# A streaming encoder step on one Trainium2 core: S5 maps all on VectorE, memory rows split by an accumulating DMA, both PSUM banks of a scan read at once

## The chip, the core and the metric

The kernel runs on one NeuronCore of a Trainium2 chip. The metric is the device time of one execution in microseconds, median of several runs. The engines in the profile are TensorE (PE, with its weight loads as PEld), VectorE (DVE), ScalarE (ACT), GpSimd (POOL) and SyncE (SP), which only issues DMAs. SBUF is the on-chip memory, PSUM the eight accumulator banks that TensorE writes.

## The reference, cut to what matters

One step of a two-layer encoder, for 512 prompt and 32 sample tokens (544 columns) of width 1024. Layer 0 mixes tokens by an S5 state-space branch (48 groups of 16 channels, 64 complex states each) with a GLU, beside a 4-head attention into 256 memory tokens; layer 1 by multi-head latent attention and the same kind of memory attention. After each comes a gated conv FFN of width 2816. What the change touches:

```python
bu_re = einsum('blgc,gnc->blgn', ug, bb_re)          # inputs to the states, complex
h_re, h_im = associative_scan(complex_affine, ...)   # h = lambda * h + bu over the tokens
y = einsum('blgn,gcn->blgc', h_re, c_re) - einsum('blgn,gcn->blgc', h_im, c_im) + d_skip * u
out = gelu(y) * sigmoid(gelu(y) @ w_glu + b_glu)

m = rms_norm(mem[None], mem_norm_g)                  # memory rows, for both layers
k, v = split(einsum('lbmd,ldk->lbmk', m, w_mem_kv))
```

## The kernel before, in words

Matmuls keep fp32 accuracy by splitting each operand into a high and a low part of a shorter type and adding three products. For weights, `weights` (L226) loads the raw block on SP's queue, ScalarE writes the high part (L231) and the negated raw block into the low part (L232), and a DMA on POOL's queue adds the raw block onto it (L233). `gemm_part` (L316) issues the three products, each on two halves of 272 columns. Three buffers exist for each of raw, high and low.

The program is written in Tile: a scheduler orders each engine's instructions by priorities from a table (ORDER, L67) that the sections of the program name with `pri` and `unit`; the engines then run their lists in that order and wait on semaphores. Pools of SBUF buffers (F, with fx merged into it; R for row pairs; BG and BS for four PSUM banks each) set how far work runs ahead. The order inside an engine's list is therefore a result of priorities, buffers and the scheduler, and a change to one place moves instructions elsewhere.

Layer 0 works over six chunks m of eight groups (loop at L1033). For each chunk, `s5_wv` (L661) builds the input maps: per real and imaginary half two products and a sum of 128x512 (L670, L672), one half on DVE and one on POOL. `s5_wvt` (L676) turns them by PE. `s5_wc` (L688) builds the output maps: per half of the groups two products and a sum of 128x576 (L697, L699), again one on DVE and one on POOL; then matmuls (L701) make the short convolution kernels, which go through POOL (L706, L708) and a DMA round trip in `s5_kernel`. `s5_scan` (L746) lets PE write two PSUM banks (L753), rotates them by four DVE operations of 128x276 (L763, L764), sums (L766, L767), scans (L771), rotates back (L774) and combines (L780, L781); two small memsets are on DVE (L758, L768). `s5_output` (L786) makes the outputs (L792, L793, transposes L804).

`mem_kv` (L333) runs between these steps as filler, in eight pieces (four blocks u of the memory rows times two layers l). A piece scales its rows by the norm's gain into a high part on ScalarE (L344) and a low part on DVE (L345), two of each of 128x256, loads a w_mkv block, and issues its matmuls (L350). Two pairs of row buffers serve the eight pieces. When all is summed, keys are finished with L398 and the transposes L404.

Then come memory attention, the GLU (L1094), the output projection, the first conv FFN, and layer 1: its norm (sums of squares L260 and L262, a chain of small DVE operations, the broadcast L284), the latents in `finish_latents`, which also multiplies the rotary tables by gains on POOL (L1216, L1218), the attention (scores L1557, transposes L1582, values L1593), the output projection and the second FFN. L324 is every weight matmul, L331 and L866 its evacuations. L966 to L968 are the evacuations of layer 0's input projection into the S5 inputs. L640 to L643 build the S5 tables by doubling, and L358 sums the squares of the memory rows on POOL.

```python
        for gh, e in enumerate((V, P)):
            g = 8 * m + 4 * gh
            for o, x in ((c, 0), (d, 1)):
                e.tensor_tensor(o[gh], view(q["cc"], [[16, 4], [0, 9], [1, 16]], 16 * (48 * x + g)),
                                view(q["prd"], [[1, 4], [48, 9], [0, 16]], 432 * x + g), ALU.mult)
            e.tensor_tensor(c[gh], c[gh], d[gh], ALU.add)
```

Of the kernel before, what the change touches and what calls it, by code (L numbers as in the profile page):

```python
# [9 lines left out]
F32 = mybir.dt.float32  # L10
F32R = mybir.dt.float32r
# [66 lines left out]
class Slots:  # L78
# [59 lines left out]
def body(ctx, tc, A, O):  # L138
# [10 lines left out]
    B = slots(pp, 8, F32, 512, "bank")  # L149
# [40 lines left out]
    B.put(b)  # L190
    F.put(warm)
# [142 lines left out]
    def mem_kv(fm, rm, bm, b1, dst):  # L334
        ps = [[bm.get(512) for _ in range(2)] for _ in range(2)]
        acc = fm.get(2, NMEM)
        for u in range(4):
            mt = fm.get(2, NMEM)
            nc.sync.dma_start(mt, A["mem"][:, 2 * u:2 * u + 2, :])
            for l in range(2):  # L340
                hi, lo = rm.get(2, NMEM), rm.get(2, NMEM)
                for k2 in range(2):
                    g = gcol("mem", l * KD + 2 * u + k2)
                    S.activation(hi[:, k2], mt[:, k2], AF.Copy, scale=g)  # L344
                    V.scalar_tensor_tensor(lo[:, k2], mt[:, k2], g, hi[:, k2].bitcast(F32), ALU.mult, ALU.subtract)  # L345
# [318 lines left out]
    def s5_wv(q, m, fs):  # L664

        a = [fs.get(4, 8, 16) for _ in range(2)]
        b = [fs.get(4, 8, 16) for _ in range(2)]
        for ri, e in enumerate((V, P)):
            for o, x, pw in ((a, ri, "pr"), (b, 1 - ri, "pi")):
                e.tensor_tensor(o[ri], view(q["bb"], [[16, 4], [0, 8], [1, 16]], 16 * (NPR * x + 4 * m)),  # L670
                                view(q[pw], [[1, 4], [NPR, 8], [0, 16]], 4 * m), ALU.mult)
            e.tensor_tensor(a[ri], a[ri], b[ri], ALU.add if ri else ALU.subtract)  # L672
        fs.put(*b)
        return a

    def s5_wvt(a, fs, bs):  # L676
        wv = []
        for ri in range(2):
            pb = bs.get(512)
            for i in range(4):  # L680
                T.transpose(pb[:, 128 * i:128 * i + 128], a[ri][:, i].rearrange("p a b -> p (a b)"), ident)
# [1120 lines left out]
```

## Time and profile before

| what | value |
|---|---|
| three runs | 1459.69, 1460.1, 1463.19 us; median 1460.1 |
| the profiled execution's own time | 1460.42 us |
| its span, first to last instruction | 1458.6 us |
| mean granted TensorE clock | 0.979 of full speed |
| busy: PE | 1409.9 us (97%) |
| busy: DVE, ACT, POOL | 738.8, 753.4, 408.7 us |
| 0 to 36.9 us: loads, first norm, start of the input projection | PE 26.66 us busy |
| 36.9 to 180.0 us: rest of the projection, S5 chunks, memory keys and values | PE 120.07, DVE 134.21 us busy |
| 180.0 to 196.5 us: last S5 output, keys, start of memory attention | PE 14.94 us busy |
| 196.5 to 690 us: memory attention, GLU, projection, first FFN | PE 492.8 us busy |
| 690 to 1010 us: layer 1 up to its attention's end | PE 313.54 us busy |
| 1010 to 1458.6 us: projection, second FFN | PE 441.84 us busy |

A busy share over the whole span mixes these stages. It is read stage by stage: where PE is busy throughout, no other engine's work shows in the time; where it is not, its waits name the engine that it waits for.

### The profile page before, as it was taken

To read this page: it belongs to the slowest core of one execution; us is meant where nothing else is said; L and a number is where in the kernel's file an instruction comes from. 1 tells how busy PE (TensorE), PEld (TensorE's weight loads), DVE (VectorE), ACT (ScalarE), POOL (GpSimd) and SP (SyncE) were. 2 spreads that over 40 slices of the span, in tenths; PEclk is the share of its full clock that TensorE was granted. 3 is DMA by queue.
4 is the path that set the end of the run, shared out by engine and by line. 5 is a ranking of instruction groups with operands and counts; after the bars stand their busy time and mean duration, and the time that the engine had idled before them with its cause. 6 is when DMAs were issued, how large, how long until landed. Compare 5 with 4: busy or idle time off the path is not lost.

```text
span 1458.6 us, 26919 instructions
## 1 busy us (share of the span) xinstructions
PE 1409.9 (97%) x10693; PEld 1315.7 (90%) x10693; DVE 738.8 (51%) x1801; ACT 753.4 (52%) x1247; POOL 408.7 (28%) x649
## 2 busy tenths in 40 slices
PE   7888899999999999999999999999999999999998
PEld 6777679999999999999989987557999999999998
DVE  7989852355513551355247755663355513551351
ACT  6455475555534553456554554654555534553452
POOL 3546532322211221124226422332322211221121
PEclk8997899999999999999999999999999999999999
DMA  8665547778888878878751342011778887888875
GB/s 246 139 145 133 118 117 161 158 175 173 175 175 174 178 173 175 176 161 184 162 132 60 97 121 48 26 30 42 163 177 175 180 176 171 178 177 171 176 155 138
DMA packets 71902, 214.77 MB, mean 147 GB/s; under 512 B 8128, under 2 KB 17312, under 8 KB 71776
## 3 DMA queue, kind: packets, MB, share of 16 engines
q0 software_dynamic: 27616, 96.16, 37.5%
q1 hardware_dynamic: 43008, 114.80, 27.1%
q10 hardware_dynamic: 1152, 2.10, 0.5%
q8 instruction: 84, 1.38, 0.4%
q14 instruction: 42, 0.34, 0.1%
HBM read 207.41 MB, written 5.61 MB: 146 GB/s over the span
## 4 chain that ended last, share of the span: by engine, by line
PE 82%; DVE 2%; issue 1%; ACT 1%; DMA 1%; POOL 0%; DVEq 0%; POOLq 0%; ACTq 0%
PE bank L324 65%; PE bank L1309 2%; PE bank L1557 2%; PE bank L1396 2%; PE bank L1593 1%; PE bank L1510 1%; PE bank L1484 1%; PE bank L1582 1%; PE bank L1192 1%; PE bank L482 1%; PE bank L520 1%; PE bank L1424 1%; DMA wlo<-i_w_f 0%; PE bank L510 0%; PE bank L1365 0%
## 5 line engine op out<-in xcount | busy, mean ns | idle before, releaser
L324 PE MATMUL bank<-rc,whi 128*128 128x272 f32 x3728 | 627.5, 289 | 0.9 <-DVE fx L393 0.7
L324 PEld LDWEIGHTS bank<-rc,whi 128*128 128x128 f32 x3728 | 528.3, 188 | 4.2 <-issue 2.1
L324 PE MATMUL bank<-rc,wlo 128*128 128x272 f32 x1864 | 388.3, 288 | 0.0
L231 ACT ACTIVATE whi<-wraw 128x1024 fp32r<-128x1024 f32 (+2 forms) x186 | 191.1, 1028 | 360.6 <-issue 314.2
L324 PEld LDWEIGHTS bank<-rc,wlo 128*128 128x128 f32 x1864 | 293.7, 188 | 1.9 <-issue 1.6
L324 PE MATMUL bank<-g,whi 128*128 128x272 f32 x1408 | 234.9, 289 | 0.0
L233 POOL DMA_DIRECT2D wlo<-i_w_f x136 | 117.3, 863 | 304.9 <-ACT wlo L232 303.0
L324 PEld LDWEIGHTS bank<-g,whi 128*128 128x128 f32 x1408 | 198.8, 188 | 0.6 <-ACT g L216 0.4
L232 ACT ACTIVATE wlo<-wraw 128x1024 fp32r<-128x1024 f32 (+2 forms) x186 | 189.0, 1016 | 9.9 <-PE bank L350 9.3
L324 PE MATMUL bank<-g,wlo 128*128 128x272 f32 x704 | 146.0, 288 | 1.6 <-DMA wlo<-i_w_f 1.6
L852 DVE SCALAR_TENSOR_TENSOR fa<-fa,gp,fa 128x546 f32<-128x546 f32 x88 | 69.4, 789 | 139.4 <-ACT fa L851 139.4
L866 DVE TENSOR_TENSOR h<-bank,h 128x272 f32<-128x272 f32 x96 | 38.2, 435 | 173.0 <-PE bank L324 172.4
L324 PEld LDWEIGHTS bank<-g,wlo 128*128 128x128 f32 x704 | 110.5, 188 | 1.9 <-DMA wlo<-i_w_f 1.9
L844 DVE TENSOR_TENSOR fa<-bank,fa 128x272 f32<-128x272 f32 x88 | 38.9, 442 | 82.6 <-PE bank L324 78.1
L851 ACT ACTIVATE fa<-fa,gp 128x546 f32<-128x546 f32 x88 | 73.1, 831 | 12.9 <-DVE fa L846 12.9
L853 DVE SCALAR_TENSOR_TENSOR fa<-fa,gp,fa 128x546 f32<-128x546 f32 x88 | 69.4, 789 | 3.1
L848 POOL COPY fa<-gp 128x2 f32<-128x2 f32 x88 | 19.0, 220 | 169.4 <-DVE g L217 105.1
L892 ACT ACTIVATE fa<-fa 128x546 f32<-128x546 f32 x44 | 29.1, 662 | 71.3 <-DVE fa L853 71.3
L849 POOL COPY fa<-fa 128x4 f32<-128x4 f32 x88 | 18.0, 204 | 166.5 <-DVE fa L846 166.5
L324 PE MATMUL bank<-ra,whi 128*128 128x272 f32 x256 | 49.5, 314 | 13.7 <-DVE fa L968 5.5
L324 PEld LDWEIGHTS bank<-ra,whi 128*128 128x128 f32 x256 | 40.5, 207 | 16.8 <-DVE fa L968 6.2
L216 ACT ACTIVATE g<-fa 128x544 fp32r<-128x544 f32 x44 | 28.9, 658 | 37.3 <-DVE fa L894 37.3
(691 smaller groups left out, 2057.2 us busy)
## 6 DMA issues: line engine op xcount, KB each, us to landing
wraw<-i_w_f SPq DMA_DIRECT2D x120, 512.0 KB
wlo<-i_w_f POOLq DMA_DIRECT2D x120, 512.0 KB, 7.3
wraw<-i_w_out SPq DMA_DIRECT2D x16, 512.0 KB
wlo<-i_w_out POOLq DMA_DIRECT2D x16, 512.0 KB, 7.4
wraw<-i_w_in SPq DMA_DIRECT2D x14, 512.0 KB
wlo<-i_w_in POOLq DMA_DIRECT2D x14, 512.0 KB, 7.5
wraw<-i_w_f SPq DMA_DIRECT2D x16, 384.0 KB
wlo<-i_w_f POOLq DMA_DIRECT2D x16, 384.0 KB, 6.1
```

The costliest lines, as they stand in the source:

```text
L231: S.activation(hi, raw, AF.Copy)
L232: S.activation(lo, raw, AF.Copy, scale=-1.0)
L233: P.dma_start(lo, ap, accum_op=ALU.add)
L324: T.matmul(ps[q][:, :c], ww, xx[:, c0:c0 + c], start=k == 0 and i == 0, stop=k == n - 1 and i == 2)
L844: V.tensor_tensor(u[:, 2:274], ps[0][:, :272], rb[:, :272], ALU.mult)
L851: S.activation(y, u[:, 2:548], AF.Identity, scale=gcol("cw", 3 * ci + 2), bias=gcol("cb", ci))
L852: V.scalar_tensor_tensor(y, u[:, 1:547], gcol("cw", 3 * ci + 1), y, ALU.mult, ALU.add)
L853: V.scalar_tensor_tensor(y, u[:, 0:546], gcol("cw", 3 * ci), y, ALU.mult, ALU.add)
L866: V.tensor_tensor(h[m][:, c0:c0 + cc], ps[qd][:, :cc], h[m][:, c0:c0 + cc], ALU.add)
L1309: T.matmul(b[:, :384], xx[:, 128 * t:128 * t + 128], ww[:, 384 * (k % 2):384 * (k % 2) + 384], start=k == 0 and i == 0, stop=k == NM - 1 a ...
L1396: T.matmul(b[:n, 256 * j:256 * j + 256], xx[:, c0:c0 + n], ww[:, k], start=k == 0 and c == 0, stop=k == 1 and c == 2)
L1557: T.matmul(b[:, :n], qt[:, 128 * t:128 * t + 128], kt[:, :n], start=True, stop=True)
```

## The change

`s5_wv` puts all six operations of a chunk on DVE, still 128x512. `s5_wc` puts its work on DVE in three operations of 128x1152, in place of three of 128x576 on each engine. Both take their buffers from a new pool FD of double width (four slots, and two made of `big`), and fx shrinks from 13 to 8. In `mem_kv`, POOL scales the rows into a new buffer `gm` (two operations of 128x256), ScalarE copies it to the high part and, negated, to the low part (128x512 each), and an accumulating DMA on POOL's queue, from SBUF to SBUF, adds `gm` onto the low part; the two DVE operations L345 of a piece go. `s5_scan` takes two adjacent banks (`get2`; the bank tiles are now 1024 wide) and reads both with one operation of 552 columns, two such in place of four; its two memsets go to POOL. The sums of squares of the first norm are all on DVE. The rotary products move from `finish_latents` to the start of layer 1. They and two small memsets of layer 1 keep their place in the program's order.

```diff
+    def get2(self):
+        for t in self.free:
+            for u in self.free:
+                a, b = t[:], u[:]
+                if a.tensor.name == b.tensor.name and b.offset == a.offset + 512:
+                    self.free = [x for x in self.free if x is not t and x is not u]
+                    return a, b, view(a, [[512, 2], [1, 512]])
+        raise AssertionError("no two banks side by side")
     def retire(self, *tiles):
...
     def slots(pool, n, dt, w, name):
...
-    B = slots(pp, 8, F32, 512, "bank")
+    B = Slots([])
+    for i in range(4):
+        t2 = pp.tile([128, 1024], F32, name=f"bank{i}")
+        for j in range(2):
+            B.free.append(t2[:, 512 * j:512 * j + 512])
+            B.own(B.free[-1])
+    banks = list(B.free)
...
             for l in range(2):
-                hi, lo = rm.get(2, NMEM), rm.get(2, NMEM)
+                hi, lo, gm = rm.get(2, NMEM), rm.get(2, NMEM), fm.get(2, NMEM)
                 for k2 in range(2):
-                    g = gcol("mem", l * KD + 2 * u + k2)
-                    S.activation(hi[:, k2], mt[:, k2], AF.Copy, scale=g)
-                    V.scalar_tensor_tensor(lo[:, k2], mt[:, k2], g, hi[:, k2].bitcast(F32), ALU.mult, ALU.subtract)
+                    P.tensor_scalar(gm[:, k2], mt[:, k2], gcol("mem", l * KD + 2 * u + k2), 0.0, ALU.mult, ALU.add)
+                S.activation(hi, gm, AF.Copy)
+                S.activation(lo, gm, AF.Copy, scale=-1.0)
+                P.dma_start(lo, gm, accum_op=ALU.add)
+                fm.put(gm)
...
-    def s5_wv(q, m, fs):
-        a = [fs.get(4, 8, 16) for _ in range(2)]
-        b = [fs.get(4, 8, 16) for _ in range(2)]
-        for ri, e in enumerate((V, P)):
+    def s5_wv(q, m, fd):
+        a, b = fd.get(2, 4, 128), fd.get(2, 4, 128)
+        for ri in range(2):
             for o, x, pw in ((a, ri, "pr"), (b, 1 - ri, "pi")):
-                e.tensor_tensor(o[ri], view(q["bb"], [[16, 4], [0, 8], [1, 16]], 16 * (NPR * x + 4 * m)),
+                V.tensor_tensor(o[:, ri].rearrange("p i (s c) -> p i s c", s=8),
+                                view(q["bb"], [[16, 4], [0, 8], [1, 16]], 16 * (NPR * x + 4 * m)),
                                 view(q[pw], [[1, 4], [NPR, 8], [0, 16]], 4 * m), ALU.mult)
-            e.tensor_tensor(a[ri], a[ri], b[ri], ALU.add if ri else ALU.subtract)
-        fs.put(*b)
+            V.tensor_tensor(a[:, ri], a[:, ri], b[:, ri], ALU.add if ri else ALU.subtract)
+        fd.put(b)
...
-    def s5_wvt(a, fs, bs):
+    def s5_wvt(a, fs, fd, bs):
...
             for i in range(4):
-                T.transpose(pb[:, 128 * i:128 * i + 128], a[ri][:, i].rearrange("p a b -> p (a b)"), ident)
+                T.transpose(pb[:, 128 * i:128 * i + 128], a[:, ri, i], ident)
...
             wv.append(w)
-        fs.put(*a)
+        fd.put(a)
...
-    def s5_wc(q, m, fs, bs):
+    def s5_wc(q, m, fs, fd, bs):
...
         pk = bs.get(512)
-        c = [fs.get(4, 9, 16) for _ in range(2)]
-        d = [fs.get(4, 9, 16) for _ in range(2)]
-        for gh, e in enumerate((V, P)):
-            g = 8 * m + 4 * gh
-            for o, x in ((c, 0), (d, 1)):
-                e.tensor_tensor(o[gh], view(q["cc"], [[16, 4], [0, 9], [1, 16]], 16 * (48 * x + g)),
-                                view(q["prd"], [[1, 4], [48, 9], [0, 16]], 432 * x + g), ALU.mult)
-            e.tensor_tensor(c[gh], c[gh], d[gh], ALU.add)
+        c, d = fd.get(8, 9, 16), fd.get(8, 9, 16)
+        for o, x in ((c, 0), (d, 1)):
+            V.tensor_tensor(o, view(q["cc"], [[16, 8], [0, 9], [1, 16]], 16 * (48 * x + 8 * m)),
+                            view(q["prd"], [[1, 8], [48, 9], [0, 16]], 432 * x + 8 * m), ALU.mult)
+        V.tensor_tensor(c, c, d, ALU.add)
+        fd.put(d)
+        for gh in range(2):
             for i in range(4):
-                T.matmul(pk[32 * i:32 * i + 32, 128 * gh:128 * gh + 128], view(q["xq"], [[1, 32]], 16 * (g + i)),
-                         c[gh][:, i, 0:8].rearrange("p a b -> p (a b)"), start=True, stop=True)
-        fs.put(*d)
+                T.matmul(pk[32 * i:32 * i + 32, 128 * gh:128 * gh + 128],
+                         view(q["xq"], [[1, 32]], 16 * (8 * m + 4 * gh + i)),
+                         c[:, 4 * gh + i, 0:8].rearrange("p a b -> p (a b)"), start=True, stop=True)
...
     def s5_scan(q, m, u, wv, fs, bs):
...
-        ps = [bs.get(512) for _ in range(2)]
+        *ps, vv = bs.get2()
...
         S.activation(mul, view(q["mag"], [[0, 2], [1, 4], [0, 70]], 4 * m), AF.Copy)
-        V.memset(view(mul, [[70, 8], [65, 2]]), 0.0)
-        cs, sn = (q["tab"][:, i, 4 * m:4 * m + 4] for i in range(2))
+        P.memset(view(mul, [[70, 8], [65, 2]]), 0.0)
         w, t0, t1 = fs.get(2, 4, 70), fs.get(2, 4, 70), fs.get(2, 4, 70)
-        for ri in range(2):
-            v = ps[ri][:, :276].rearrange("p (a b) -> p a b", a=4)
-            V.tensor_tensor(t0[:, ri, :, 1:], v, cs[:, :, 1:], ALU.mult)
-            V.tensor_tensor(t1[:, ri, :, 1:], v, sn[:, :, 1:], ALU.mult)
+        P.memset(w[:, :, :, 0:1], 0.0)
+        for t, i in ((t0, 0), (t1, 1)):
+            V.tensor_tensor(t[:, :, :, 1:], view(vv, [[512, 2], [69, 4], [1, 69]]),
+                            view(q["tab"], [[0, 2], [70, 4], [1, 69]], 70 * (NPR * i + 4 * m) + 1), ALU.mult)
...
         V.tensor_tensor(w[:, 1, :, 1:], t0[:, 1, :, 1:], t1[:, 0, :, 1:], ALU.subtract)
-        V.memset(w[:, :, :, 0:1], 0.0)
...
     for k in range(2, KD):
-        (V if k % 2 else P).tensor_tensor(sqs[k % 2], sqs[k % 2], sqs[k], ALU.add)
+        V.tensor_tensor(sqs[k % 2], sqs[k % 2], sqs[k], ALU.add)
...
     lr = exr.enter_context(tc.tile_pool(name="l0b", bufs=1, reuse_waits="tile"))
-    R, fx = slots(lr, 4, F32R, 512, "rb"), slots(lr, 13, F32, FW, "fx")
+    R, fx, FD = slots(lr, 4, F32R, 512, "rb"), slots(lr, 8, F32, FW, "fx"), slots(lr, 4, F32, 2 * FW, "fd")
...
     F.merge(fx)
-    F.merge(Slots([big[:, FW * i:FW * i + FW] for i in range(NX)]))
+    FD.merge(Slots([big[:, 2 * FW * i:2 * FW * i + 2 * FW] for i in range(2)]))
...
     qsT = [lp.tile([96, 128], F32, name=f"qsT{g}") for g in range(3)]
+    kcs = lp.tile([128, 320], F32, name="kcs")
+    for i, nm in enumerate(("cos", "sin")):
+        for o, nr in ((view(kcs, [[32, 5], [1, 32]], 160 * i), "kr"), (gcs[:, i], "qr")):
+            tc.keep_in_program_order(P.tensor_tensor(o, view(cn, [[32, 5], [1, 32]], CN[nm][0]),
+                                                     view(grow(nr), [[0, 5], [1, 32]]), ALU.mult))
...
     ssl = lp.tile([128, 10], F32, name="ssl")
-    V.memset(ssl[:, 8:10], 1.0)
+    tc.keep_in_program_order(V.memset(ssl[:, 8:10], 1.0))
...
                         view(r1, [[1, 5], [0, 2]]), ALU.mult)
-        kcs = lp.tile([128, 320], F32, name="kcs")
-        for i, nm in enumerate(("cos", "sin")):
-            P.tensor_tensor(view(kcs, [[32, 5], [1, 32]], 160 * i), view(cn, [[32, 5], [1, 32]], CN[nm][0]),
-                            view(grow("kr"), [[0, 5], [1, 32]]), ALU.mult)
-            P.tensor_tensor(gcs[:, i], view(cn, [[32, 5], [1, 32]], CN[nm][0]), view(grow("qr"), [[0, 5], [1, 32]]),
-                            ALU.mult)
...
     def key_norms():
         ss = sm(108, "kss", 1)
-        V.memset(ss, 1.0)
+        tc.keep_in_program_order(V.memset(ss, 1.0))
```

The rest passes the pools on to the functions (FD to `s5_wv`, `s5_wvt` and `s5_wc`) and gives the output maps back to FD. Line numbers of the new kernel are higher by 15 to 19.

How this moves instructions stands in the engines' lists. The first place is POOL's list at the start of the S5 chunks (`cc`, `bb`: output and input factors; `pr`, `pi`, `prd`: powers; `wlo`: low weight parts; `rb`: row pairs; `kp`: kernels). Before:

```order
L1218 TENSOR_TENSOR gcs<-cn,gr 128x160
L697 TENSOR_TENSOR fa_73<-cc_396,prd 128x576
L670 TENSOR_TENSOR fa_76<-bb_395,pi 128x512
L670 TENSOR_TENSOR fa_74<-bb_395,pr 128x512
L697 TENSOR_TENSOR fx_853<-cc_396,prd 128x576
L672 TENSOR_TENSOR fa_74<-fa_74,fa_76 128x512
L699 TENSOR_TENSOR fa_73<-fa_73,fx_853 128x576
L697 TENSOR_TENSOR fa_92<-cc_396,prd 128x576
L697 TENSOR_TENSOR fx_853<-cc_396,prd 128x576
L699 TENSOR_TENSOR fa_92<-fa_92,fx_853 128x576
L233 DMA wlo_99<-i_w_in 128x1024
```

Now:

```order
L360 TENSOR_SCALAR fx_853<-fx_852,gp 128x256 x2
L250 DMA wlo_97<-i_w_in 128x1024
L363 DMA rb_846<-fx_853 128x512
L250 DMA wlo_95<-i_w_in 128x1024
L250 DMA wlo_96<-i_w_in 128x1024
L250 DMA wlo_97<-i_w_mkv 128x1024
L250 DMA wlo_95<-i_w_mkv 128x1024
L250 DMA wlo_96<-i_w_mkv 128x1024
L726 TENSOR_TENSOR kp<-kp,fa_72 128x2x16
L724 TENSOR_TENSOR fa_72<-cn,sp_141 128x32
L250 DMA wlo_97<-i_w_mkv 128x1024
L360 TENSOR_SCALAR fx_854<-fx_852,gp 128x256 x2
```

The map products are gone from POOL; in their stead stand scalings (L360), accumulating row DMAs (L363), weight issues (L250, which was L233) and memsets of the scan (L776), one behind the other.

The second place is PE's list at the end of S5, where `L793` and `L792` are the last chunk's outputs, `L350` the last memory matmuls and `L404` the transposes of the keys. Before:

```order
L792 MATMUL bank_63<-fx_861,big 69x128
L404 MATMUL bank_68<-cn,fa_71 128x128 x4
L350 MATMUL bank_65<-whi_96,rb_852 128x512
L793 MATMUL bank_63<-fx_853,fx_860 69x128
L792 MATMUL bank_63<-fx_861,big 69x128
L793 MATMUL bank_63<-fx_853,fx_860 69x128
L792 MATMUL bank_63<-fx_861,big 69x128
L793 MATMUL bank_63<-fx_853,fx_860 69x128
L430 MATMUL bank_68<-cn,fa_74 128x2 x4
```

Now, where L808 and L809 were L792 and L793, L423 was L404, L820 was L804 and L341 was L324:

```order
L808 MATMUL bank_65<-fa_67,fa_70 69x128
L809 MATMUL bank_65<-big,fx_856 69x128
L808 MATMUL bank_65<-fa_67,fa_70 69x128
L809 MATMUL bank_65<-big,fx_856 69x128
L341 MATMUL bank_63<-rc_1876,whi_94 128x272 x2
L341 MATMUL bank_63<-rc_1877,whi_94 128x272 x2
L820 MATMUL bank_66<-cn,fx_852 128x69 x4
L423 MATMUL bank_65<-cn,fx_855 128x128 x4
L341 MATMUL bank_63<-rc_1876,wlo_97 128x272
L820 MATMUL bank_66<-cn,fa_68 128x69 x4
```

The transposes of the keys moved behind the last output matmuls and behind four weight matmuls.

The third place is PE's list at the start of layer 1, from the sums of squares to the broadcast. Before (the lines left out are L324 as well):

```order
L260 MATMUL bank_67<-cn,fa_72 128x1 x4
L262 MATMUL bank_67<-cn,fa_72 32x1 x4
L324 MATMUL bank_65<-rc_1903,whi_96 128x272
L324 MATMUL bank_68<-rc_1903,whi_96 128x272
L324 MATMUL bank_65<-rc_1904,whi_96 128x272
L324 MATMUL bank_68<-rc_1904,whi_96 128x272
...
L324 MATMUL bank_65<-rc_1909,wlo_99 128x272
L284 MATMUL bank_70<-cn,nr_0_306 128x128 x4
L285 MATMUL bank_63<-cn,nr_0_306 128x32
```

Now (L277 and L279 are the sums, L301 and L302 the broadcast):

```order
L277 MATMUL bank_64<-cn,fa_75 128x1 x4
L279 MATMUL bank_64<-cn,fa_75 32x1 x4
L341 MATMUL bank_63<-rc_1876,whi_92 128x272
L301 MATMUL bank_66<-cn,nr_0_302 128x128 x4
L302 MATMUL bank_65<-cn,nr_0_302 128x32
L341 MATMUL bank_63<-rc_1877,whi_92 128x272
L341 MATMUL bank_63<-rc_1876,wlo_95 128x272
```

Before, 23 weight matmuls stood between the sums and the broadcast; now one does.

## Rows read from the trace of the kernel before

**Rows 1.** Windows: us; busy of PE, PEld, DVE, ACT, POOL; PE clock; DMA share; GB/s.

```profile
36.90:180.00 143.10, 120.07 (x975) 102.87 (x976) 134.21 (x230) 74.65 (x158) 78.82 (x73) 0.87 0.57 132
180.00:196.50 16.50, 14.94 (x114) 12.72 (x112) 11.63 (x56) 12.37 (x32) 4.26 (x8) 1.00 0.54 146
230.00:690.00 460.00, 459.91 (x3646) 457.85 (x3643) 193.80 (x387) 236.94 (x287) 102.39 (x178) 1.00 0.80 174
```

**Rows 2.** Waits of PE, 36.9 to 180 us: us in total, times, longest.

```profile
PE bank L324 <- DVE fa L968: 5.5, 3, 3.6
PE bank L350 <- DVE rb L345: 3.9, 4, 1.7
PE bank L701 <- DVE fa L699: 3.5, 1, 3.5
```

**Rows 3.** Timeline of DVE, 62 to 87 us: start, us, line, operation.

```profile
62.83 0.68 DVE L670 TENSOR_TENSOR big<-bb,pi 128x512 f32<-128x512 f32 x1
63.43 0.95 DVE L640 TENSOR_TENSOR big<-tab,p_sc 128x768 f32<-128x768 f32 x1
...
86.05 0.44 DVE L763 TENSOR_TENSOR fx<-bank,tab 128x276 f32<-128x276 f32 x1
86.41 0.43 DVE L764 TENSOR_TENSOR fx<-bank,tab 128x276 f32<-128x276 f32 x1
```

**Rows 4.** Timeline of DVE, 48 to 64 us.

```profile
52.32 1.33 DVE L640 TENSOR_TENSOR big<-tab,p_sc 128x96 f32<-128x96 f32 x1
...
54.95 0.43 DVE L966 TENSOR_TENSOR fa<-bank,fa 128x272 f32<-128x272 f32 x1
```

**Rows 5.** Timeline of POOL, the same time.

```profile
51.81 1.74 POOL L672 TENSOR_TENSOR fa<-fa,fa 128x512 f32<-128x512 f32 x1
...
54.88 1.23 POOL L697 TENSOR_TENSOR fa<-cc,prd 128x576 f32<-128x576 f32 x1
```

**Rows 6.** Lines by form, DVE, 36.9 to 180 us: busy us, mean ns | idle.

```profile
L345 DVE SCALAR_TENSOR_TENSOR rb<-fa,gp,rb 128x256 fp32r<-128x256 f32 x12 | 8.7, 737 | 0.0
```

**Rows 7.** Lines by form, POOL, 36.9 to 180 us.

```profile
L697 POOL TENSOR_TENSOR fx<-cc,prd 128x576 f32<-128x576 f32 x7 | 10.1, 1442 | 2.4 <-DVE rb L345 2.3
L233 POOL DMA_DIRECT2D wlo<-i_w_mkv x8 | 7.0, 875 | 11.3 <-ACT wlo L232 10.7 <-issue 0.3 <-ACT fa L806 0.3
...
L358 POOL TENSOR_TENSOR fx<-fx,fx 128x512 f32<-128x512 f32 x2 | 3.3, 1674 | 0.0
...
L699 POOL TENSOR_TENSOR big<-big,fx 128x576 f32<-128x576 f32 x1 | 1.9, 1912 | 0.0
```

**Rows 8.** Timeline of POOL, 204 to 208 us.

```profile
204.93 0.48 POOL L498 TENSOR_SCALAR fa<-fa,zri 128x256 f32<-128x256 f32 x1
```

**Rows 9.** Timeline of DVE, line 1094.

```profile
205.68 0.93 DVE L1094 SCALAR_TENSOR_TENSOR fa<-fa,fa 128x544 f32<-128x544 f32 x1 [0.21 <-ACT fa L1092]
...
213.88 0.72 DVE L1094 SCALAR_TENSOR_TENSOR fa<-fa,fa 128x544 f32<-128x544 f32 x1
```

**Rows 10.** Lines by form, ACT, 36.9 to 180 us.

```profile
L344 ACT ACTIVATE rb<-fa,gp 128x256 fp32r<-128x256 f32 x12 | 5.8, 506 | 2.8 <-PE bank L350 2.0 <-DVE rb L345 0.9
```

**Rows 11.** DMA issues, 0 to 250 us: count, KB each, median us to landing.

```profile
wlo<-i_w_mkv POOLq DMA_DIRECT2D x8, 512.0 KB, 7.1
...
o_mem_k<-fa POOLq DMA_DIRECT2D x1, 256.0 KB, 2.5
```

**Rows 12.** Timeline of PE at the end of S5.

```profile
186.33 0.63 PE L404 MATMUL bank<-cn,fa 128*128 128x128 f32 x4 [0.93 <-DVE fa L398]
```

**Rows 13.** Timeline of PE at the start of layer 1.

```profile
695.07 0.24 PE L262 MATMUL bank<-cn,fa 128*32 128x1 f32 x8
...
698.23 0.60 PE L284 MATMUL bank<-cn,nr 128*128 128x128 f32 x4
```

**Rows 14.** Windows in and at the end of layer 1's attention, columns as in rows 1.

```profile
740.00:990.00 250.00, 243.61 (x1555) 188.94 (x1553) 155.10 (x532) 131.91 (x357) 88.15 (x153) 0.98 0.25 69
990.00:1010.00 20.00, 19.93 (x104) 12.43 (x104) 8.87 (x33) 7.96 (x24) 3.69 (x9) 1.00 0.00 0
```

More of the change, by code (lines that the diff above doesn't have):

```diff
@@ L190, in body @@
     B.put(b)
+    B.free = banks
     F.put(warm)
@@ L792, in s5_output @@
                 T.matmul(o, u[:, 4 * gh + i, :], kk[gh][:, i], start=True, stop=False)
-                T.matmul(o, hh[:, 4 * gh + i, 0:69], wc[gh][:, i, 1:9].rearrange("p a b -> p (a b)"), start=False,
+                T.matmul(o, hh[:, 4 * gh + i, 0:69], wc[:, 4 * gh + i, 1:9].rearrange("p a b -> p (a b)"), start=False,
                          stop=True)
@@ L916, in body @@
     R = slots(lr, 16, F32R, NT, "ra")
-    NX = 4
-    big = lp.tile([128, NX * FW], F32, name="big")
+    big = lp.tile([128, 4 * FW], F32, name="big")
     BG, BS = B.take(4), B.take(4)
@@ L982, in out0 @@
         yield from s5_output(us[m], wc, kk, hs[m], y, F, BS)
-        F.put(us[m], hs[m], *wc, *kk)
+        F.put(us[m], hs[m], *kk)
+        FD.put(wc)
         ys.append(y)
@@ L1023, in products @@
         with pri("s5_wv"):
-            return s5_wv(q5, m, F)
+            return s5_wv(q5, m, FD)
     def turn(a):
         with pri("s5_wvt"):
-            wvs.append(s5_wvt(a, F, BS))
+            wvs.append(s5_wvt(a, F, FD, BS))
     def step(g):
@@ L1038, in do_wc @@
         with pri("s5_wc"):
-            wcs.append((s5_wc(q5, m, F, BS), s5_kernel(q5, m, F)))
+            wcs.append((s5_wc(q5, m, F, FD, BS), s5_kernel(q5, m, F)))
     do_wc(0)
@@ L1068, in body @@
     P.dma_start(O["ssm"], q5["hf"])
-    F.retire(big, *fxs)
+    F.retire(*fxs)
     exr.close()
```

## Prediction, made before the changed kernel was run

> **What bounds the kernel now.** I began with the windows by stage. TensorE (PE) is busy 97% of the whole span, so the time can only go down where PE stands idle or at a low clock. The first conv FFN leaves it next to nothing: 459.9 of 460 us, 0.126 us a matmul [rows 1]. The stretch from 36.9 us (row scales ready) to 180.0 us (last scan instruction) is another matter: PE is busy 120.1 of 143.1 us, at a granted clock of 0.87, while VectorE (DVE) is busy 134.2 us, 94% [rows 1]. The waits of PE in this stretch say on whom: the three longest entries, 12.9 us together, are all ended by DVE results [rows 2]. So DVE bounds this stretch.
>
> Then I asked why DVE is so busy. Where POOL runs nothing beside it, the distance from one start to the next is 0.60 us for 512 columns and 0.36 for 276 [rows 3]: about 0.07 us plus 1 us per 960 columns. Laid over each of the 230 instructions that DVE ran in the stretch (scans at 1.25), that sums to 94.4 us; busy were 134.2. Some 40 us are stretching. The timeline shows by what: an operation of 96 columns takes 1.33 us and ends with POOL's three-operand instruction beside it (52.32 + 1.33 = 53.65; 51.81 + 1.74 = 53.55), while 272 columns whose first operand is PSUM take 0.43, as ever, beside POOL's next one of the kind [rows 4, 5]. A group repeats it: L345, 0.34 by that rule, means 0.74 over 12 [rows 6]. POOL's map products, 36 in the stretch at some 1.4 us, the longest of 1.9 [rows 7], are the blockers.
>
> **The change part by part.** *Maps on DVE.* DVE takes over POOL's half. The products of s5_wv stay 512 wide, 36 instead of 18: +18 x 0.60 = +10.9 us. Those of s5_wc become 18 of 1152 columns (0.07 + 1.20 = 1.27 us) in place of 18 of 576 (0.67): 22.9 - 12.1 = +10.8. *Scan.* Twelve reads of 552 columns from PSUM (0.645) replace 24 of 276 (0.36): 7.7 - 8.6 = -0.9. Twelve memsets move to POOL; they are tiny and taken as 0. *Low parts.* Sixteen L345 leave DVE: 16 x 0.34 = -5.4. Sum +15.4: DVE's own work in the stretch goes from 94.4 to 109.8 us.
>
> Against that stands the stretching. The 36 products leave POOL, some 50 us of its 78.8 [rows 1, 7]. What stays or comes and can block: 16 scalings of 256 columns, 0.48 us alone [rows 8], 7.7 us, and three L358 of about 1.6 [rows 7], 4.8 us; together 12.5. The bounds are 0 and 12.5; since DVE also reads PSUM or waits part of the time, I take the middle, 6.
>
> The Trainium skill ("SBUF — State Buffer", section "Who interferes with whom") says that a DVE instruction with two SBUF inputs and a GpSimd instruction that reads SBUF contend, the later one fully blocked, and that one with at most one SBUF input, outside the 2-port modes, does not: [rows 4, 5] agree. It speaks against a part of this change, since the new POOL scalings read SBUF; by it nearly the whole 12.5 would be charged. That is rival (b), from the rows alone.
>
> DVE idled 143.1 - 134.2 = 8.9 us in the stretch [rows 1]. Now the scan waits in addition for two memsets that stand in POOL's queue behind weight issues of 0.88 us, which wait for ScalarE's negated copy [rows 7]; I put idling at 12. So 109.8 + 6 + 12 = 128 instead of 143: **-15 us**. PE allows it: its idle time there is 143.1 - 120.1 = 23.0 us [rows 1], before any gain of clock.
>
> *The low parts' new way.* For each of the eight pieces: two POOL scalings (0.96), two ScalarE copies of 512 columns where there were two of 256 at 0.51 [rows 10] (up to 1.0 each if time went with width), one issue of 0.88 [rows 7], and the landing of 256 KB. No transfer of this kind is in the trace; its nearest rows are 2.5 us for 256 KB written out and 7.1 for the accumulating 512 KB [rows 11]. I take 4 us, nearer the half-size accumulating one: a chain of about 8 us. Beside it run 512 KB of w_mkv low parts with their 7.1 us, issued at about the same place and needed by the same matmuls, so I charge nothing; without that cover each piece would cost PE its excess, rival (c). SP's queue keeps its order. ScalarE gains up to 8 us on 74.7 of 143.1 [rows 1], also nothing.
>
> *End of S5.* Before, the transposes L404 stood ahead of the last output matmuls and waited 0.93 us for DVE [rows 12]; now they stand behind these. PE is busy 14.94 of 16.5 us here [rows 1], so 0 to 1.6 can be gained: **-1**.
>
> *Start of layer 1.* Between the sums of squares (L262) and the broadcast (L284), 23 projection matmuls cover DVE's chain of small operations. In the new order one stands there. PE would wait from 695.07 + 0.24 = 695.31 to 698.23, 2.9 us, less one matmul [rows 13]: **+2.7**; 0 if the 22 displaced ones fill some of the 6.4 us of idleness that PE has from 740 to 990 us [rows 14].
>
> *End of layer 1's attention.* Before, 31 of the output projection's matmuls lay between the last score and value matmuls (990 to 1009 us), where PE was busy 19.93 of 20 us [rows 14]; two are left. The 29 covered at most 29 x 0.126 = 3.7: 0 to +4, taken **+2**.
>
> *Costed at nothing:* the sums of squares on DVE at the front (the matmuls behind them wait for weights of 7 us' landing, [rows 11]), and the rotary products, which POOL loses in the stretch and gets in layer 1, where it has room.
>
> Sum: -15 - 1 + 2.7 + 2 = -11.3. The profiled execution took 1460.4 us, 1.8 more than its span and 0.3 more than the median of 1460.1. So 1460.4 - 11.3 = 1449.1, **1448.8** set against the median. A measurement of this kernel can tell about 0.3%, 4.4 us: faster is below 1455.7, slower above 1464.5.
>
> **The rivals.**
> (a) *PE binds first.* PE runs its list in order, and of its 23 us of idleness half may only change owner, from DVE to ScalarE or a landing. Then some 10 are gained in the stretch: -10 - 1 + 4.7 = -6.3, 1454.
> (b) *POOL's scalings block in full.* 12.5 in place of 6: -8.5 - 1 + 4.7 = -4.8, 1455. For it: [rows 4, 5] show a whole instruction waited out, and a 544-column operation took 0.93 us beside a POOL scaling, 0.72 without [rows 8, 9]. Against it: that was 0.21 us of loss, not 0.48.
> (c) *The low parts come late; slower.* There are two pairs of row buffers, so a piece cannot run far ahead, and POOL issues in order: a scaling or an accumulating issue behind a weight issue that waits for its buffer is late itself, and so are the scan's memsets behind it. Each of eight pieces then stops PE by chain minus cover. At 3 us apiece that is 24: -15 + 24 - 1 + 4.7 = +12.7, 1473. It decides from 2 us a piece (8 x 2 = 16 against 15 + 1 - 4.7 + 4.4). For it: PE already waited 3.9 us for the old low rows, four times [rows 2]. Against it: the cover of 7.1 us.
> (d) *The stretching is not POOL's; slower.* If DVE keeps its ratio of 134.2 to 94.4, 109.8 becomes 156, plus 9 to 12 of idling: +23 - 1 + 4.7, 1487. Against it are [rows 4, 5].
> (e) *Layer 1 gives more back.* Its order differs in more places than the two costed; twice the 4.7 and half the gain of the stretch make it 1460.4 - 7.5 - 1 + 9.4 = 1461, no change that can be told.
> That the change does not do what it says holds for one part: s5_wv's products are no wider. That is in the sum.
>
> **How the numbers follow.** Chances: forecast 0.56, (a) 0.12, (b) 0.10, (c) 0.10, (d) 0.03, (e) 0.09. The forecast counts as faster; (a) and (b) lie near the bound, 0.19 of their 0.22 faster; (e) is mostly the same, and (c) under its point too. That makes faster 0.75, same 0.13, slower 0.12. The range: with no blocking and idling unchanged the stretch is 109.8 + 8.9 = 118.7, -24, which PE's 23.0 of idleness caps; with layer 1 at nothing that ends at 1437, so 1438 is the low end. At the other, blocking 12.5 and idling 15 make 137, -6; no gain at S5's end and +6.7 in layer 1 reach 1461. I end at 1459, which leaves out (c), (d) and a part of (e).
>
> **What would show it.** Right: s5_wv's products on DVE start 0.60 us apart and s5_wc's 1.27; POOL is busy under 35 us in the stretch; the last scan operation falls at about 165 us; PE's waits for DVE there halve. In layer 1 there is a wait of 2 to 3 us before the broadcast at its start. Wrong: PE waiting for the low rows' landing more than 2 us a piece (c), products of 512 columns at over 1 us with POOL idle (d), or an unchanged end of the stretch with DVE idle (a).

## The result: 5.3% slower, and the profile after

The changed kernel takes 1539.35 us, median of four runs (1535.98 to 1541.17), against 1461.57 before: a ratio of 1.053, 95% interval 1.0504 to 1.0556. It is far outside the range, and on the other side. The profiled execution's span is 1536.2 us, 77.6 more.

Its page begins so:

```profile
span 1536.2 us, 26902 instructions
...
PE 1450.9 (94%) x10693; PEld 1331.6 (87%) x10693; DVE 709.7 (46%) x1782; ACT 755.7 (49%) x1247; POOL 378.6 (25%) x646
...
PEclk8988999999999999999999799898999999999999
```

PE issues the same 10693 instructions, but is busy 41 us longer (1409.9 before) and idle 85.3 us instead of 48.7. Part of the longer busy time is the clock: its mean is 0.968 of full speed instead of 0.979. Taken over the spans that is 49 us of full-speed time given up instead of 31, so some 18 of the 41 us (an estimate); what the rest is isn't shown. The PEclk line shows where the clock is lower: behind the middle, in layer 1. At the front both kernels have low slices.

To see where the time went I cut both spans at the same work: at 36.9 us, at the end of the last scan operation (180.0 us in both kernels; it starts at 179.6), the first evacuation of the first FFN (L844 before, L860 now), the sums of squares of layer 1, the first matmul on L1510 (now L1525), and the last value matmul. The windows of the changed kernel, columns as in [rows 1]:

```profile
36.90:180.00 143.10, 115.80 (x964) 98.70 (x965) 113.11 (x209) 75.47 (x155) 44.90 (x64) 0.90 0.62 139
180.00:312.50 132.50, 124.56 (x893) 112.43 (x892) 51.64 (x143) 73.61 (x140) 37.57 (x52) 0.97 0.62 141
312.50:715.00 402.50, 397.92 (x3145) 394.88 (x3145) 167.54 (x354) 202.76 (x243) 88.59 (x164) 1.00 0.80 172
715.00:896.10 181.10, 171.58 (x1225) 158.52 (x1223) 92.30 (x273) 87.14 (x192) 60.38 (x89) 0.94 0.42 108
896.10:1075.50 179.40, 157.98 (x731) 92.62 (x730) 86.57 (x323) 78.61 (x232) 44.26 (x87) 0.91 0.09 21
1075.50:1536.20 460.70, 454.42 (x3574) 449.11 (x3573) 172.58 (x372) 213.00 (x252) 92.60 (x165) 1.00 0.75 164
```

And of the kernel before, the ones not yet shown, cut at the same work:

```profile
180.00:297.30 117.30, 115.08 (x872) 105.93 (x871) 49.28 (x141) 71.99 (x137) 36.86 (x51) 1.00 0.66 150
297.30:694.20 396.90, 396.90 (x3150) 396.57 (x3149) 172.94 (x343) 201.30 (x240) 84.40 (x160) 1.00 0.81 174
694.20:863.60 169.40, 165.34 (x1249) 155.53 (x1247) 95.66 (x284) 89.99 (x196) 61.04 (x90) 0.97 0.48 121
863.60:1008.90 145.30, 142.90 (x779) 90.26 (x778) 83.54 (x323) 77.79 (x232) 44.34 (x87) 1.00 0.11 26
1008.90:1458.60 449.70, 442.94 (x3526) 441.55 (x3525) 176.67 (x372) 213.96 (x252) 89.96 (x165) 1.00 0.78 168
```

By stage that is 0.0 (S5), +15.2 (keys, memory attention, GLU), +5.6 (first FFN), +11.7 (layer 1's front), +34.1 (its attention) and +11.0 (the rest), in all +77.6. In S5, DVE was relieved as forecast, from 134.2 to 113.1 us busy, and nothing came of it: not one of PE's waits there is on DVE any more, but PE idles 27.3 us where it idled 23.0. The larger part lies in layer 1, whose code the change hardly touches. In the attention stage PE does 48 instructions fewer, is idle 21.4 us instead of 2.4, and its granted clock falls from 1.00 to 0.91. What PE waits for in these two places of the changed kernel (waits in us in total, times, longest; first S5, then 992 to 1075.5 us):

```profile
PE bank L369 <- ACT rb L361: 4.7, 2, 4.0
PE bank L369 <- DMA rb<-fa: 4.4, 1, 4.4
PE bank L758 <- ACT fa L759: 4.1, 1, 4.1
PE bank L700 <- ACT fa L702: 3.5, 2, 2.9
PE bank L341 <- ACT rb L362: 2.1, 1, 2.1
...
PE bank L369 <- DMA rb<-fx: 1.7, 1, 1.7
...
PE bank L1572 <- ACT fa L512: 3.4, 2, 1.9
PE bank L1572 <- ACT fe L1577: 2.4, 2, 1.7
PE bank L1597 <- ACT fn L1577: 1.5, 2, 1.1
```

L361 and L362 are ScalarE's copies of the memory rows, `rb<-fa` and `rb<-fx` the landing of their low parts. The second place has an odd row: a score matmul (L1572) waits for ScalarE's exponentials of the *memory* attention (L512), with which it shares no data. No such row exists before. That led to the theories.

### The profile page after: what moved, and what is told of

Read it like the earlier page. It is cut to its first block, busy times and chain, and to the rows that moved or that the text cites. A ratio compares the mean times of both kernels' runs of the same rounds, so it can differ in the third digit from the quotient of the medians.

```text
span 1536.2 us, 26902 instructions
## 1 busy us (share of the span) xinstructions
PE 1450.9 (94%) x10693; PEld 1331.6 (87%) x10693; DVE 709.7 (46%) x1782; ACT 755.7 (49%) x1247; POOL 378.6 (25%) x646
## 3 DMA queue, kind: packets, MB, share of 16 engines
q10 hardware_dynamic: 1152, 2.10, 0.4%
## 4 chain that ended last, share of the span: by engine, by line
PE 42%; DVE 3%; ACT 3%; issue 2%; DMA 1%; POOL 0%; DVEq 0%; ACTq 0%; POOLq 0%
PE bank L341 28%; PE bank L1324 2%; PE bank L1608 2%; PE bank L1572 2%; PE bank L1597 1%; PE bank L1525 1%; PE bank L1411 1%; DMA wlo<-i_w_f 1%; PE bank L1499 1%; PE bank L1213 1%; PE bank L1439 1%; PE bank L1380 1%; PE bank L539 0%; PE bank L501 0%; ACT fn L1577 0%
## 5 line engine op out<-in xcount | busy, mean ns | idle before, releaser
L341 PE MATMUL bank<-rc,whi 128*128 128x272 f32 x3728 | 637.2, 290 | 4.4 <-ACT fa L1171 2.1
L341 PEld LDWEIGHTS bank<-rc,whi 128*128 128x128 f32 x3728 | 534.6, 189 | 12.0 <-ACT fa L1171 3.5
L341 PE MATMUL bank<-rc,wlo 128*128 128x272 f32 x1864 | 400.0, 289 | 0.4 <-DMA wlo<-i_w_f 0.3
L341 PEld LDWEIGHTS bank<-rc,wlo 128*128 128x128 f32 x1864 | 299.1, 189 | 1.2 <-DMA wlo<-i_w_f 0.5
L341 PE MATMUL bank<-g,whi 128*128 128x272 f32 x1408 | 241.7, 290 | 0.9 <-ACT g L233 0.4
L341 PEld LDWEIGHTS bank<-g,whi 128*128 128x128 f32 x1408 | 202.0, 188 | 4.7 <-DVE h L882 1.1
L250 POOL DMA_DIRECT2D wlo<-i_w_f x136 | 117.4, 863 | 311.3 <-ACT wlo L249 304.4
L341 PE MATMUL bank<-g,wlo 128*128 128x272 f32 x704 | 151.7, 288 | 2.0 <-DMA wlo<-i_w_f 2.0
L341 PEld LDWEIGHTS bank<-g,wlo 128*128 128x128 f32 x704 | 112.6, 188 | 2.7 <-DMA wlo<-i_w_f 2.7
L860 DVE TENSOR_TENSOR fa<-bank,fa 128x272 f32<-128x272 f32 x88 | 35.7, 438 | 152.7 <-PE bank L341 152.7
L868 DVE SCALAR_TENSOR_TENSOR fa<-fa,gp,fa 128x546 f32<-128x546 f32 x88 | 67.9, 791 | 59.9 <-ACT fa L867 59.8
L869 DVE SCALAR_TENSOR_TENSOR fa<-fa,gp,fa 128x546 f32<-128x546 f32 x88 | 66.8, 789 | 0.9
L341 PE MATMUL bank<-ra,whi 128*128 128x272 f32 x256 | 48.0, 312 | 5.1 <-ACT whi L258 3.0
L234 DVE TENSOR_TENSOR g<-fa,g 128x544 fp32r<-128x544 f32 x44 | 31.9, 726 | 35.3 <-ACT g L233 34.7
L341 PEld LDWEIGHTS bank<-ra,whi 128*128 128x128 f32 x256 | 40.6, 209 | 6.8 <-ACT whi L258 4.4
```

The costliest lines, as they stand in the source:

```text
L234: V.tensor_tensor(lo, src, hi.bitcast(F32), ALU.subtract)
L250: P.dma_start(lo, ap, accum_op=ALU.add)
L341: T.matmul(ps[q][:, :c], ww, xx[:, c0:c0 + c], start=k == 0 and i == 0, stop=k == n - 1 and i == 2)
L860: V.tensor_tensor(u[:, 2:274], ps[0][:, :272], rb[:, :272], ALU.mult)
L868: V.scalar_tensor_tensor(y, u[:, 1:547], gcol("cw", 3 * ci + 1), y, ALU.mult, ALU.add)
L869: V.scalar_tensor_tensor(y, u[:, 0:546], gcol("cw", 3 * ci), y, ALU.mult, ALU.add)
```

## The experiments

**Theory W**: four double-width PSUM tiles in place of eight single ones are the cause. The scheduler keeps its dependences so that an instruction on one half of such a tile waits for readers of the other half. **Theory M**: the memory rows' new low parts come late (rival (c)), and all else follows. Rival P: the S5 stretch is bound by PE or ScalarE anyway.

### e1: single-width banks again

```diff
-    B = Slots([])
-    for i in range(4):
-        t2 = pp.tile([128, 1024], F32, name=f"bank{i}")
...
+    B = slots(pp, 8, F32, 512, "bank")
-        *ps, vv = bs.get2()
+        ps = [bs.get(512) for _ in range(2)]
```

> The change, but with the eight PSUM banks as eight tiles of 512 again and the scan reading them one by one (four operations of 276). Theory W (the double-width bank tiles make the scheduler order layer 1 and the memory attention worse): layer 1 takes its 764 us again instead of 821, and the part from the last scan to the FFN its 117 instead of 132, so 1539 - 57 - 15, about 1467, and 1455 to 1475. Theory M (the low parts' new chain is what costs): the order of layer 1 would be as in the change, 1520 to 1540.

Measured: 1457.22 us, ratio 0.9962 (0.9947 to 0.9977), as W said. The whole loss is gone and a small gain is there. Theory M falls as the main cause: the new low parts are in this kernel. The edit takes away the joint reads too, and with them the scan's two memsets go back to VectorE, so this run alone does not tell the tile from the reads; e2 and e11 do.

### e2: the kernel before with double-width banks, and nothing else

```diff
-    B = slots(pp, 8, F32, 512, "bank")
+    B = Slots([])
+    for i in range(4):
+        t2 = pp.tile([128, 1024], F32, name=f"bank{i}")
...
```

> The kernel before, with nothing changed but the PSUM banks being halves of four tiles of 1024; every instruction is as before, the scan still reads bank by bank. Theory W: most of the loss comes with this alone, 1461 + 57 to 1461 + 72, 1515 to 1535. Theory M: no change, 1458 to 1465.

Measured: 1564.27 us, ratio 1.0689 (1.0662 to 1.0716). The direction is W's; the size is more than it said, 102 us instead of at most 72, and more than the whole change loses. Between 715 and 860 us this kernel's waits of PE begin with:

```profile
PE bank L331 <- ACT fa L1157: 16.4, 6, 3.2
PE bank L1316 <- POOL wlo L1293: 2.1, 5, 0.5
```

L331 is the weight matmul, L1157 the square that ScalarE takes of an earlier query block. Six times the first matmul of a block waits 2 to 3 us for it:

```profile
742.05 0.82 PE L331 MATMUL bank<-rc,whi 128*128 128x272 f32 x2 [3.21 <-ACT fa L1157]
...
752.69 0.82 PE L331 MATMUL bank<-rc,whi 128*128 128x272 f32 x2 [2.93 <-ACT fa L1157]
```

Whether these are waits for the neighbour can be read from the built programs, which hold every semaphore wait and every operand's tile and offset. I took each wait, looked up the instruction that raises the semaphore to the value waited for, and counted the pairs that have no bank and no buffer in common, but the two halves of one bank tile:

```
                    waits of PE for a neighbour bank's user    of other engines
before                 0                                           0
e2                   361 (245 on VectorE, 116 on ScalarE)         92
the change           359 (245 and 114)                            67
e1                     0                                           0
e6                    51 (4 and 47)                                5
e11                    0                                           0
```

All six waits of L331 for L1157 are among the 361, and six of L1572 for L512 among the 359. The scheduler orders by the same dependences, so the order changes too: in e2, as in the change, one matmul stands in layer 1's first norm where 23 did, and two of the output projection's lie inside the attention where 48 did. In e1, e6 and e11 the counts are 23 and 48 again. How the loss divides between waiting and order isn't separated here; both come with the tile.

### e3: the old low parts, with double-width banks

```diff
-                    P.tensor_scalar(gm[:, k2], mt[:, k2], ...)
-                S.activation(hi, gm, AF.Copy)
-                S.activation(lo, gm, AF.Copy, scale=-1.0)
-                P.dma_start(lo, gm, accum_op=ALU.add)
+                    S.activation(hi[:, k2], mt[:, k2], AF.Copy, scale=g)
+                    V.scalar_tensor_tensor(lo[:, k2], mt[:, k2], g, hi[:, k2].bitcast(F32), ...)
```

> The change with the memory rows' high and low parts made as before (ScalarE high, VectorE low, no POOL scaling, no accumulating DMA from SBUF). Theory W: layer 1 stays at 821 us; in the S5 stretch PE loses its 14 us or so of waits for ScalarE's copies and for the landing, DVE gets 5.4 us back: 1520 to 1535. Theory M: 1455 to 1475.

Measured: 1526.78 us, ratio 1.044 (1.041 to 1.0471). As W said; the last scan operation starts at 165.0 us instead of 179.6. So in the change the new low parts do cost some 13 us, which answers the rows above on L361, L362 and on the landing. The S5 stretch of this kernel:

```profile
36.90:165.40 128.50, 114.40 (x985) 96.86 (x983) 117.54 (x229) 77.37 (x163) 30.08 (x44) 0.96 0.61 144
```

It is 14.6 us shorter than before and than in the change: with the old low parts VectorE's relief comes through in S5, even with the wide tiles. The time is then lost again behind it: the first FFN's evacuation begins at 299.8 us, against 297.3 before.

### e4: single-width banks and the old low parts

The diffs of e1 and e3 together, and one buffer less in F.

> Narrow banks and the old low parts together (one buffer of 576 less in the pool F, else it doesn't fit), so what is left of the change is the maps on VectorE, the sums of squares on VectorE, and the rotary products' place. Theory W: the relief of VectorE comes through, 143 us of the S5 stretch becoming 130 to 135: 1448 to 1456. Rival P (PE or ScalarE binds the stretch anyway): 1458 to 1465. Theory M says the same as W here.

Measured: 1462.65 us, ratio 0.9999 (0.9985 to 1.0013): Rival P's number, though not by its mechanism. The last scan operation is 9.1 us earlier (170.5), but the first FFN's evacuation begins at 297.2, where it did. PE's largest wait in total from 37 to 300 us, and the windows of 10 us around the end of S5:

```profile
PE bank L801 <- DMA fa<-kd: 8.1, 7, 2.6
```

```profile
160.00:170.00 10.00, 8.60 (x88) 6.80 (x84) 7.95 (x28) 5.99 (x16) 2.31 (x4) 1.00 0.83 176
170.00:180.00 10.00, 6.51 (x47) 5.30 (x48) 7.30 (x26) 7.13 (x21) 2.26 (x4) 1.00 0.52 158
180.00:190.00 10.00, 7.86 (x32) 6.46 (x32) 5.06 (x23) 1.86 (x3) 1.73 (x3) 0.51 0.53 131
190.00:200.00 10.00, 10.00 (x50) 8.34 (x48) 3.85 (x18) 3.72 (x9) 1.66 (x3) 0.64 0.08 29
200.00:210.00 10.00, 9.44 (x63) 7.52 (x63) 5.35 (x16) 7.54 (x21) 4.41 (x9) 1.00 0.10 18
```

The S5 outputs now wait for the loads of the short-convolution kernels. PE is busy 6.5 of 10 us, and then the granted clock falls to 0.51, the lower level, for some 10 us in which the keys and the memory attention begin. Before, it was 1.00 there [rows 1]. The two windows at 0.51 and 0.64 give up 4.9 + 3.6 = 8.5 us of full-speed time (an estimate), about what S5 had gained. The kernel before gives up its clock inside S5 instead: 0.87 over the stretch, against 0.91 here.

### e5: e1 once more, for its trace

> The kernel of e1_narrow_banks once more, since its profiled execution was a disturbed one. Theory W with relief: 1455 to 1459 again; the last scan operation at about 170 us instead of 179.6, as in e4_narrow_old_low, and PE's waits there on something else than VectorE's products.

Measured: 1456.94 us, ratio 0.9951 (0.9928 to 0.9973). The last scan operation falls at 172.7 us, and of PE's waits from 36.9 to there all but 0.4 us are on ScalarE and on DMAs; that 0.4 us is on VectorE's maps. The largest:

```profile
PE bank L362 <- ACT rb L354: 4.9, 1, 4.9
PE bank L741 <- ACT kp L718: 4.8, 1, 4.8
PE bank L803 <- DMA fa<-kd: 3.4, 2, 1.9
PE bank L764 <- ACT fa L695: 2.5, 2, 2.1
```

So without the wide tiles, with the new low parts, the stretch gives 143.1 - 136.2 = 6.9 us, not 15. In this execution 5.5 us of it are lost again between 398 and 739 us; e8 asks why.

### e6: double-width tiles in S5 only

```diff
+    pw = exs.enter_context(tc.tile_pool(name="psw", bufs=1, space=PSUM))
+    B = slots(pp, 4, F32, 512, "bank")
+    for i in range(2):
+        t2 = pw.tile([128, 1024], F32, name=f"wide{i}")
...
     ex.close()
+    exs.close()
+    BS = slots(pn, 4, F32, 512, "bnk")
```

> The change whole, its scans reading two banks at once, but only four banks are halves of double-width tiles, and these tiles live only until the S5 part is over; the other four, and all eight from the memory attention on, are tiles of 512. Theory W (a wait for the neighbour bank's reader is what costs, through the whole program): like e1_narrow_banks, 1452 to 1462, with layer 1 back at 764 us. Rival J (reading two banks at once is itself what costs): 1500 or more.

Measured: 1470.96 us, ratio 1.0061 (1.0038 to 1.0085), between the two, and outside what either said. From the first FFN on it runs like before; the last scan operation is at 187.2 us, the first FFN's evacuation at 308.9 instead of 297.3. Its 51 neighbour waits are all in S5, and it is 14 us behind e1. Either W works in small, or the joint read costs; e11 decides.

### e7: the new low parts alone

The kernel before with the four lines of e3 the other way round.

> The kernel before with only the memory rows' new low parts. If these help by themselves (VectorE's 16 operations gone while POOL still blocks it): 1450 to 1457. If they help only where POOL is free of maps: 1459 to 1468. Rival (c) of the prediction, late low parts: 1470 or more.

Measured: 1469.12 us, ratio 1.0037 (1.0024 to 1.005). It lies between the bands. With POOL still at its maps the low parts hurt. The pair e1 and e4 has them gain about 5 (1457 against 1463, one buffer apart), with POOL freed and narrow tiles; with POOL freed and wide tiles they cost 13 (e3). What makes the difference isn't isolated.

### e8: the rotary products alone

The kernel before with the products moved to the start of layer 1, as in the change.

> The kernel before with only the rotary products (and two small memsets) at the start of layer 1. In e5_narrow_again the first FFN and layer 1's start, from 398 to 739 us, took 5.5 us longer than before, around the place where these products now run. If they are the cause: 1463 to 1468. If not (and POOL blocks VectorE 3 us less in the S5 stretch): 1457 to 1462.

Measured: 1461.62 us, ratio 0.9999 (0.9984 to 1.0014). No effect, as costed. What held up e5's first FFN is open; in e11 the same stretch takes 335.5 us, against 335.9 before.

### e9 and e10: the kernels' loads on two queues; their maps at a more urgent priority

```diff
-                nc.sync.dma_start(kk[gh][:, i], ...)
+                (nc.sync, nc.scalar)[gh].dma_start(kk[gh][:, i], ...)
```

> The kernel of e1_narrow_banks with half of the loads of the short-convolution kernels (kk from kd) issued on ScalarE's queue, half on SP's, so that the eight of a chunk are issued in about 3 us instead of 6. If PE's 6.4 us of waits for these loads hold back the end of S5: 1451 to 1455. If the chain behind them (keys, memory attention) ends last anyway: 1455 to 1459. ScalarE issuing may also cost it: up to 1460.

```diff
-         "s5_input": 260, "norm0": 20, ..., "s5_wc": 10,
+         "s5_input": 260, "norm0": 20, ..., "s5_wc": -70,
```

> The kernel of e1_narrow_banks with the output maps and short-convolution kernels of a chunk (s5_wc) at a more urgent priority (-70 instead of 10). If the loads of the kernels are late because their maps are: 1450 to 1455. If VectorE's earlier maps only push the scans back: 1457 to 1465.

Measured, both on top of e1's kernel: 1467.43 us (1.0042, 1.0025 to 1.0059) and 1466.61 us (1.0024, 1.0008 to 1.004). Both miss: the last scan operation is at 176.1 us in either, later than e5's 172.7. PE's waits for the kernels' loads, 6.4 us up to 300 us in e5, are still 4.8 and 4.4, and others grow: in e9 PE waits 8.6 us for ScalarE's evacuations of the S5 outputs (L808), in e10 10.5 us for its row copies (L354), where e5 had 4.9.

### e11: one double-width tile, for the scans alone

```diff
+    B.merge(slots(pw, 2, F32, 512, "bnk"))
+    t2 = pw.tile([128, 1024], F32, name="wide0")
...
-            hs.append(s5_scan(q5, m, us[m], wvs[m], F, BS))
+            hs.append(s5_scan(q5, m, us[m], wvs[m], F, BW))
```

> The change whole, scans reading two banks at once, but with one double-width tile alone, kept for the scans; the other six banks are tiles of 512 (S5's other work has two of them where it had four with the scans). No instruction waits for a neighbour bank's reader in this program. Theory W: the 14 us that e6_wide_in_s5_only is slower than e1_narrow_banks go, 1452 to 1460. Rival J (the joint read itself, which holds both banks until the second product is through): still 1468 to 1475. Rival B (too few banks for the rest of S5): 1460 to 1470, with PE waiting there on ScalarE's evacuations.

Measured: 1458.58 us, ratio 0.9976 (0.996 to 0.9991), as W said. The change's every operation is there, the joint reads too, and the loss is gone; no instruction waits for a neighbour, and the counts in layer 1's order are the old ones (e2's table and the text under it). Rival J falls. Rival B's time doesn't show, but S5 itself gains only 2.4 us (last scan operation at 177.2), and PE waits there for ScalarE, 13.7 us for the row copies (L363) alone.

### e12: three pairs of row buffers

```diff
-    R, fx, FD = slots(lr, 4, F32R, 512, "rb"), ...
+    R, fx, FD = slots(lr, 6, F32R, 512, "rb"), ...
```

> The kernel of e1_narrow_banks with three pairs of row buffers for the memory rows in place of two, so that a piece's scaling, copies and landing can start one piece earlier. In e5_narrow_again PE waited 4.9 us for ScalarE's copy of the rows and 1.1 for their landing. If the late low parts (rival (c) of the prediction, by a small amount) are what holds the S5 stretch now: 1449 to 1454. If PE's other waits take their place: 1454 to 1459. If the pieces that run ahead keep ScalarE from the S5 evacuations: 1459 to 1466.

Measured: 1455.31 us, ratio 0.9948 (0.9929 to 0.9968). It can't be told from e1 (0.9962) or e5 (0.9951), and PE's wait for ScalarE's copy of the rows is still there, 4.8 us where e5 had 4.9. So the third pair did not make these rows earlier, and whether they hold the stretch stays open. Any of the three is faster than both kernels of the study.

## Why the prediction was wrong, step by step

- **What bounds the kernel, and the stretching**: right. The new kernel's VectorE starts its products 0.60 us apart and those of 1152 columns 1.27, as worked out:

```profile
63.27 0.68 DVE L688 TENSOR_TENSOR big<-bb,pr 128x512 f32<-128x512 f32 x1
63.87 0.68 DVE L688 TENSOR_TENSOR big<-bb,pi 128x512 f32<-128x512 f32 x1
...
67.99 1.35 DVE L715 TENSOR_TENSOR fd<-fd,fd 128x1152 f32<-128x1152 f32 x1
69.26 0.68 DVE L688 TENSOR_TENSOR big<-bb,pi 128x512 f32<-128x512 f32 x1
```

  DVE's busy time, 113.1 us, is close to the 109.8 + 6 of the sum.
- **The low parts, "so I charge nothing"**: this step failed, and took all that the stretch was to give. The landing took 5.4 us, not 4, and PE's waits for L361, L362 and the landing sum to 12.9 us (4.7 + 4.4 + 2.1 + 1.7), 1.6 a piece, just under the 2 at which rival (c) decides; e3 gives 13 us.

```profile
rb<-fa POOLq DMA_DIRECT2D x5, 256.0 KB, 5.4
```

- **"So 109.8 + 6 + 12 = 128"**: DVE idles 143.1 - 113.1 = 30.0 us in the change, not 12. In e3, with the old low parts, the stretch is 128.5 us and the idling 128.5 - 117.5 = 11.0, and the last scan operation starts at the forecast 165 us. That the total agrees is partly luck: the sixteen L345 are back in e3 (5.4 us), and about as much is saved on the stretching, 117.5 - 109.8 - 5.4 = 2.3 instead of 6, and on the idling. With narrow tiles and the new low parts (e5) the idling is 136.2 - 113.2 = 23.0 and 6.9 us of the 15 are left, which rival (a), "half may only change owner", describes. With 6.9 in place of 15 the sum would have ended at 1457, within the range. What bounds the stretch once DVE is relieved differs from run to run and is not isolated.
- **End of S5, -1**: the stage from there to the first FFN lost 15.2 us. **Layer 1, +2.7 and +2**: the first was about right by itself: PE stands idle 2.1 us at that place in the change, and the broadcast starts 2.6 us after the sums. But the wait that the trace names there is a neighbour's (the one matmul left, for ScalarE's square L1171), and the stages of layer 1 lost 57 us together. Here lies the main failure of the prediction. I read the new order at three places, found filler gone from each, and costed that as matmuls displaced within a program otherwise the same. I did not ask why the order of layer 1 should change when layer 1's code hardly does. The term "*Scan.*", 7.7 - 8.6 = -0.9, took the joint banks for a matter of twelve reads, where the edit redefines the tile of every PSUM access in the program. e2 shows what that costs: 102 us.
- **Rival (e)**, layer 1 giving back more, had the right place and no mechanism, and so the wrong size. **Rival (d)** is refuted: DVE was busy 113.1 us, not 156. **Rival (b)**, scalings that block in full, did not show in DVE's time, 113.1 - 109.8 = 3.3 us; its effect is on the other side, where POOL's own scalings were stretched.

## What to carry to other kernels

Where a framework derives waits from tiles, as here, the tile is the unit of waiting: two buffers joined into one for a single wide read then wait for each other wherever either is used. Join them for the stage and the use that need it, and compare the count of waits, or the order in a stage that the edit does not touch, before and after. If far-off order changes, find out why before costing it. And the relief of one engine is worth only what the work moved elsewhere leaves of it: here 14.6 us in S5 with the old low parts and nothing with the new ones.

## What the runs showed that I had not expected

The stretching between VectorE and POOL is seen both ways. In the change, POOL's scalings of 256 columns take three to four times as long where VectorE works beside them as in the group of 471 ns, four from 166.2 to 168.0 us, beside which VectorE ran nothing. Its groups by form from 36.9 to 180.7 us (mean ns):

```profile
L360 POOL TENSOR_SCALAR fa<-fa,gp 128x256 f32<-128x256 f32 x6 | 8.4, 1409 | 5.3 <-DMA fa<-i_mem 5.3
...
L360 POOL TENSOR_SCALAR fx<-fx,gp 128x256 f32<-128x256 f32 x2 | 4.2, 2086 | 1.2 <-PE bank L758 1.2
...
L360 POOL TENSOR_SCALAR fa<-fx,gp 128x256 f32<-128x256 f32 x4 | 1.8, 471 | 3.3 <-DMA fx<-i_mem 3.3
```

POOL was busy 44.9 us in the stretch, where the prediction said under 35. And an earlier end of one stage can be lost again behind it: in e4, 10 us with PE busy 6.5 were followed by 10 at a granted clock of 0.51, and the first FFN began when it had before.
